# First mixer: the pool's columns of the input projection ahead of the recurrence's

## The chip, the cores and the metric

The kernel runs on one core of one Trainium2 chip. The metric is the device time of one execution in microseconds. The kernel before took 1364.03 us (median of 3 runs, 1363.72 to 1364.52).

## What is computed

Two blocks of a network work on 256 tokens of width 1024. The first block begins with a mixer of three branches, and only this mixer is touched by the change. The reference, cut to it:

```python
h = rms_norm(x, g_mix_pre[l])
(lru_x, lru_gate, pool_in, q, k, v, q_idx, k_idx, w_idx,
 gate_logits) = split_columns(h @ w_in[l], IN_SIZES)     # 512, 512, 512, 512, 64, 64, 512, 64, 8, 3072
ua = causal_depthwise_conv(lru_x, conv_w[l], conv_b[l])
ya = rg_lru(ua, ...) * jax.nn.gelu(lru_gate)             # recurrence over the tokens
yb = multiscale_pool(pool_in, w_pool[l], pool_scale[l])  # means over windows of 2, 4, 8, 16 tokens, then a 128x128 product per group
yc = dsa_attention(q, k, v, q_idx, k_idx, w_idx)         # attention over the top 64 keys
up = jnp.einsum('bsnc,ncd->bsnd', jnp.stack([ya, yb, yc], axis=2), w_branch[l])
gates = jax.nn.sigmoid(gate_logits.reshape(bsz, s, N_BRANCH, D_MODEL) + b_gate[l])
merged = jnp.sum(gates * up, axis=2)
```

Behind it come the mixer's output projection, an attention over a memory, a feed-forward part, and a second block of two layers with a token mixer and 32 experts each.

## The kernel before

The mixer is `mixer1`. The normed input stands transposed in `hT`, split into a high and a low part (`hTh`, `hTl`). Weights are loaded by SyncE's queue (SP) in tiles of 1 MB (`load_w`, L224), and each half of a tile is split into a high part by ScalarE (`whi`, L239) and a low part by VectorE (`wlo`, L241). The pool `whl` has three buffers for such a pair. `halves` hands the pairs out in the order of a list (`cols`, then `order`) and issues one split ahead. A **unit** (L287) is one product of 128 output columns: 8 × 3 matmuls of 256 tokens (L277 to L279), and a copy by ScalarE.

`main` (L532) is a generator that runs the units in order: four for the index queries `iT`, four for the queries `qT`, four for `lru_x`, four for `lru_g`, four for `poolT`, and then for each branch n in the order 1 (pool), 0 (recurrence), 2 (attention), twice: four gate units, and two products of the branch with `w_branch` (24 matmuls each, in the order of the branch's four column groups g0 to g3 or k0 to k3, for two column blocks). It yields after each.

Beside it run up to three **chains**, also generators, kept in one list: `dsa` (attention, L702), `lru` (recurrence, L827) and `pooling` (L786). After each yield of `main` the chains get one step and two steps in turn (L596); `step` (L155) always takes the chain at the head of the list and puts it at the end. `dsa` is started after the first `qT` unit, `lru` after the first `lru_g` unit, `pooling` after the last `poolT` unit. In front of the first product of a branch, `finish` (L170) steps all chains round until that branch's chain is at its end; no unit of `main` is issued in between.

One group k of `lru` is five steps: the convolution (L822, L824) and a square; the matmuls for its two gates (L856, 8 of them) and their Tanh (L860, L861); the decay (L867 to L872); a Sqrt (L875, L876); then L878, L879, the scan over the tokens (L880), L881 and the split of the result into `yh` (L882) and, at the head of the next step, `yl` (L884). The tiles `lua`, `lz`, `lr`, `li`, `la` and `lt` have one buffer each. One group g of `pooling` is g + 1 additions (L804), L811 to L813, a product (L815, two matmuls in the trace), and the split (L795, L796). `dsa` first makes scores and picks keys for both halves of the tokens, then for each half and each half of the heads: products (L759, four matmuls in the trace at a time, "quad" below), scaling (L753), a softmax (L694 to L700), transposes (L769), a product with the values (L778) and the split (L782, L784).

The framework waits and allocates by itself and orders each engine's instructions by priority in the order of the source; an instruction that isn't ready in its reckoning can be passed by later ones. The engines take their instructions in the order so made.

Of the kernel before, what the change touches and what calls it, by code (L numbers as in the profile page):

```python
# [138 lines left out]
class Net:  # L139
# [339 lines left out]
    def mixer1(self, ph):  # L479
# [5 lines left out]
        with tc.tile_pool(name="pxn", bufs=1, reuse_waits="tile") as pxn:  # L485
            xn = self.normed(pxn, "n1")
            hT = self.hpair(ph, 8)
# [5 lines left out]
        s1 = cp.enter_context(tc.tile_pool(name="ps1", bufs=1, reuse_waits="tile"))  # L493
        A4 = lambda name: s1.tile([P, 4, S], F32, name=name, tag="A4", bufs=7)
        ys = [Split(*[s1.tile([P, 4, S], F32R, name="y%s%d" % (q, n)) for q in "hl"]) for n in range(3)]
# [15 lines left out]
        for src, dst in ((kv_raw[:, :, 0:64], kT), (iw_raw[:, :, 0:64], kiT)):  # L511
            W = self.hl_tiles(KT, 128)
            for d in range(2):
# [6 lines left out]
        self.unit(W, hT, self.copy_to(vw), m=72)  # L520

        cols = ([2176 + 256 * n for n in range(2)] + [1536 + 256 * n for n in range(2)]
                + [256 * n for n in range(6)])
        order = []
        for n in (1, 0, 2):
            for half in range(2):
# [2 lines left out]
        hs = self.halves([(win[:, c:c + 256], KT, 256, "n") for c in cols] + order)  # L529
        tmp = {}  # L530

        def main():  # L532
            for j in range(4):
                self.unit(next(hs), hT, self.copy_to(iT[:, j]))
                if j == 0:
                    bk = self.bank()
                    for tt in range(2):
                        self.nc.tensor.transpose(bk[:, tt * 72:(tt + 1) * 72], vw[:, tt * P:(tt + 1) * P], self.ident[:72, :72])
                    act.activation(vtok, bk[:, :144].rearrange("p (t n) -> p t n", t=2), AF.Copy)
                yield  # L540
            for j in range(4):
                self.unit(next(hs), hT, self.copy_to(qT[:, j]))
                if j == 0:
                    tmp["dsa"] = self.start(self.dsa(s1, A4, qT, kT, iT, kiT, vtok, ys[2]))
                yield
            lru_x = s1.tile([P, 4, 3 + S], F32, name="lru_x")
            lru_g = A4("lru_g")
            poolT = s1.tile([P, 4, 16 + S], F32, name="poolT")
            v.memset(lru_x[:, :, 0:3], 0.0)
            v.memset(poolT[:, :, 0:16], 0.0)  # L550
            for j in range(4):
                self.unit(next(hs), hT, self.copy_to(lru_x[:, j, 3:]))
                yield
            for j in range(4):
                self.unit(next(hs), hT, self.copy_to(lru_g[:, j]))
                if j == 0:
                    tmp["lru"] = self.start(self.lru(s1, lru_x, lru_g, ys[0]))
                yield
            for j in range(4):
                self.unit(next(hs), hT, self.copy_to(poolT[:, j, 16:]))  # L560
                yield
            tmp["pool"] = self.start(self.pooling(s1, poolT, ys[1]))
            for n in (1, 0, 2):
                for half in range(2):
                    g = A4("gates")
                    for i in range(4):
                        j = n * 8 + half * 4 + i
                        self.unit(next(hs), hT, lambda b: act.activation(g[:, i], b, AF.Tanh, bias=bg[:, j:j + 1], scale=0.5))
                        yield
                    if half == 0:  # L570
                        self.finish(tmp[{1: "pool", 0: "lru", 2: "dsa"}[n]], fill=0)
                    for f2 in range(2):
                        W = next(hs)
                        bk = self.bank()
                        for f in range(2):
                            self.feat(bk[:, f * S:(f + 1) * S], W, f * P, P, ys[n])
                        k0 = half * 4 + f2 * 2
                        gg = g[:, f2 * 2:f2 * 2 + 2]
                        b = bk.rearrange("p (f t) -> p f t", f=2)
                        m = merged[:, k0:k0 + 2]  # L580
                        if n == 1:
                            v.scalar_tensor_tensor(m, gg, 1.0, b, op0=OP.add, op1=OP.mult)
                        else:
                            v.scalar_tensor_tensor(gg, gg, 1.0, b, op0=OP.add, op1=OP.mult)
                            v.tensor_tensor(m, m, gg, op=OP.add)
                        if n == 2:
                            if k0 == 0:
                                tmp["mT"] = self.hpair(ph, 8)
                            mT = tmp["mT"]
                            sl = slice(k0, k0 + 2)  # L590
                            act.activation(mT.hi[:, sl], m, AF.Copy, scale=0.5)
                            v.scalar_tensor_tensor(mT.lo[:, sl], m, 0.5, mT.hi[:, sl], op0=OP.mult, op1=OP.subtract)
                        yield

        for i, _ in enumerate(main()):
            self.step(1 + i % 2)  # L596
# [9 lines left out]
        with c:  # L606
            hs = self.halves(self.w_chunks(A["w_out"][0], KT))
# [1356 lines left out]
```

## Time and profile before

| | before |
|---|---|
| median of 3 runs | 1364.03 us |
| the profiled execution: its own time | 1362.82 us |
| the profiled execution: span of its instructions | 1360.9 us |
| TensorE busy (matmul) | 1246.7 us (92%) |
| VectorE busy | 702.4 us (52%) |
| ScalarE busy | 552.3 us (41%) |
| mean granted TensorE clock | 0.957 |

The span runs from the first to the last instruction. Busy time is the time in which an instruction of the engine runs; overlapping ones count once. TensorE's matmuls are pipelined, so that a busy TensorE isn't one at its peak. The mixer takes the first 220 us or so of the span, and the change touches the stretch from about 50 us on.

### The profile page before, as it was taken

How to read it: one execution, taken by the hardware profiler on the slowest of the kernel's cores; microseconds unless marked ns; L12 is line 12 of the kernel's file. 1: busy time of each engine (PE TensorE's matmuls, PEld its weight loads, DVE VectorE, ACT ScalarE, POOL GpSimd, SP SyncE). 2: the span in 40 equal slices, each digit the busy share in tenths (PEclk: the TensorE clock that was granted, in tenths of full speed). 3: DMA queues.
4: the chain of work that ended last, by engine and by line, in shares of the span. 5: the costliest groups of instructions: out<-in, count | busy, mean ns of one | idle time of the engine just before them, and what ended most of it. 6: DMA issues, size and time to landing. Idle time of an engine off the chain costs nothing. (4 is left out here: it accounts for less than half of the span.)

```text
span 1360.9 us, 26539 instructions
## 1 busy us (share of the span) xinstructions
PE 1246.7 (92%) x11058; PEld 999.5 (73%) x11058; DVE 702.4 (52%) x1414; ACT 552.3 (41%) x1022; POOL 76.8 (6%) x91
## 2 busy tenths in 40 slices
PE   6999999999999999999989977788999989978886
PEld 6988899866999995788876645465888877645553
DVE  5797756545555554686563322225685553332324
ACT  5578546544444443445532211114345532211212
POOL 2000000000000001122100000001122100000000
PEclk9998999999999998999989999888999989998988
DMA  9553448769955555864368999999563476999994
GB/s 313 166 180 96 167 159 275 303 269 379 365 201 188 186 186 180 296 228 152 142 278 364 418 418 419 418 420 336 175 229 139 171 279 281 418 418 418 418 418 181
DMA packets 131946, 375.93 MB, mean 276 GB/s; under 512 B 7056, under 2 KB 90128, under 8 KB 100848
## 3 DMA queue, kind: packets, MB, share of 16 engines
q1 hardware_dynamic: 130080, 367.84, 71.8%
q0 software_dynamic: 1312, 5.21, 1.0%
q8 instruction: 90, 1.47, 0.4%
q10 hardware_dynamic: 432, 1.14, 0.2%
q14 instruction: 32, 0.26, 0.1%
HBM read 373.12 MB, written 1.05 MB: 275 GB/s over the span
## 5 line engine op out<-in xcount | busy, mean ns | idle before, releaser
L241 DVE TENSOR_TENSOR wlo<-w,whi 128x1024 fp32r<-128x1024 f32 x214 | 263.0, 1231 | 190.0 <-ACT whi L239 189.7
L239 ACT ACTIVATE whi<-w 128x1024 fp32r<-128x1024 f32 x214 | 225.7, 1057 | 269.4 <-PE bk L278 181.2
L277 PE MATMUL bk<-hTh,whi 128*128 128x256 f32 (+1 forms) x1128 | 321.8, 287 | 2.7 <-ACT whi L239 2.5
L278 PE MATMUL bk<-hTl,whi 128*128 128x256 f32 (+1 forms) x1128 | 317.2, 282 | 0.9 <-DVE hTl L384 0.7
L279 PE MATMUL bk<-hTh,wlo 128*128 128x256 f32 (+1 forms) x1128 | 316.3, 281 | 0.3 <-DVE wlo L241 0.2
L277 PEld LDWEIGHTS bk<-hTh,whi 128*128 128x128 f32 (+1 forms) x1128 | 211.5, 188 | 21.4 <-issue 4.1
L1631 PE MATMUL bk<-w,XT 128*32 128x256 f32 (+1 forms) x2816 | 178.1, 410 | 44.9 <-DMA w<-in_w_up 41.0
L278 PEld LDWEIGHTS bk<-hTl,whi 128*128 128x128 f32 (+1 forms) x1128 | 210.9, 187 | 3.4 <-DVE hTl L384 1.2
L279 PEld LDWEIGHTS bk<-hTh,wlo 128*128 128x128 f32 (+1 forms) x1128 | 210.8, 187 | 2.0 <-DVE kk L1421 0.8
L1631 PEld LDWEIGHTS bk<-w,XT 128*32 128x32 f32 x2816 | 100.2, 118 | 121.6 <-issue 72.6
L1760 PE MATMUL bk<-Sg,xn 128*128 128x128 f32 x704 | 90.1, 285 | 4.3 <-DVE Sg L1740 4.3
L1760 PEld LDWEIGHTS bk<-Sg,xn 128*128 128x128 f32 x704 | 87.6, 201 | 6.8 <-issue 5.3
L1815 PE MATMUL bk<-w,hd 128*32 x704 | 79.8, 593 | 9.1 <-DMA w<-in_w_down 5.4
L1803 ACT ACTIVATE hd<-bk 128x256 f32<-128x256 f32 x22 | 8.4, 384 | 192.3 <-PE bk L1801 192.3
L1766 DVE TENSOR_SCALAR XT<-bk,gp,modcol 128x128 f32<-128x128 f32 x88 | 36.1, 410 | 87.3 <-PE bk L1760 79.0
L1822 ACT ACTIVATE oh<-od 128x512 fp32r<-128x512 f32 x44 | 27.7, 629 | 88.0 <-DVE od L1821 88.0
L1815 PEld LDWEIGHTS bk<-w,hd 128*32 128x32 f32 x704 | 23.4, 110 | 53.2 <-issue 49.6
L1793 DVE SCALAR_TENSOR_TENSOR mth<-mth,cslot,bk 128x256 f32<-128x256 f32 x22 | 10.6, 481 | 90.6 <-PE bk L1631 90.6
L1764 ACT ACTIVATE XT<-bk,modcol,gp 128x128 f32<-128x128 f32 x88 | 40.1, 456 | 37.0 <-DVE XT L1766 37.0
L1055 PE MATMUL ada<-w,cact 128*32 128x512 f32 x384 | 52.4, 654 | 1.0 <-DMA w<-in_w_ada 1.0
L1821 DVE TENSOR_TENSOR od<-bk,gb 128x512 f32<-128x512 f32 x44 | 30.2, 687 | 36.0 <-PE bk L1815 36.0
L1823 DVE TENSOR_TENSOR ol<-od,oh 128x512 fp32r<-128x512 f32 x44 | 30.4, 691 | 31.6 <-ACT oh L1822 31.5
(511 smaller groups left out, 1938.1 us busy)
## 6 DMA issues: line engine op xcount, KB each, us to landing
w<-in_w_gate SPq DMA_DIRECT2D x64, 1024.0 KB, 19.9
w<-in_w_up SPq DMA_DIRECT2D x64, 1024.0 KB, 19.9
w<-in_w_down SPq DMA_DIRECT2D x64, 1024.0 KB, 19.9
w<-in_w_in SPq DMA_DIRECT2D x48, 1024.0 KB, 6.6
w<-in_w_ada SPq DMA_DIRECT2D x48, 1024.0 KB, 5.0
w<-in_w_ffn_in SPq DMA_DIRECT2D x22, 1024.0 KB, 11.5
w<-in_w_out SPq DMA_DIRECT2D x12, 1024.0 KB, 5.3
w<-in_w_ffn_out SPq DMA_DIRECT2D x11, 1024.0 KB, 6.8
```

Source lines behind the costliest of these rows:

```text
L239: self.nc.scalar.activation(W.hi, v, AF.Copy)
L241: self.nc.vector.tensor_tensor(W.lo, v, W.hi, op=OP.subtract)
L277: mm(out, l.hi, r.hi, start=start, stop=False)
L278: mm(out, l.hi, r.lo, start=False, stop=False)
L279: mm(out, l.lo, r.hi, start=False, stop=stop)
L1055: te.matmul(bk[q * 32:(q + 1) * 32, :], cact[:, k:k + 1].to_broadcast([P, 32]), w[:, q * 512:(q + 1) * 512], start=k == 0, stop=k == KT - 1)
L1631: self.nc.tensor.matmul(out[ps, :S], XT[:, k, ps], w[i][:, k * S:(k + 1) * S], start=k == 0, stop=k == KT - 1)
L1760: te.matmul(o, xn[:, tt, d], Sg[:, tt], start=tt == 0, stop=tt == 1)
L1764: act.activation(XT[:, d], o, AF.Identity, scale=gp[:, d:d + 1], bias=bp[:, d:d + 1])
L1766: v.tensor_scalar(XT[:, d], o, gp[:, d:d + 1], bp[:, d:d + 1], op0=OP.mult, op1=OP.add)
L1815: te.matmul(bks[h][ps, :], hd[:, f, ps], wds[i][:, f * D + h * 512:f * D + h * 512 + 512], start=f == 0, stop=f == 1)
L1823: v.tensor_tensor(o.lo, t, o.hi, op=OP.subtract)
```

## The change

The units of the pool's columns go ahead of those of `lru_x` and `lru_g`, the columns of `w_in` are loaded in that order, and `pooling` is started between them. `lru_g` is allocated after that.

```diff
         cols = ([2176 + 256 * n for n in range(2)] + [1536 + 256 * n for n in range(2)]
-                + [256 * n for n in range(6)])
+                + [256 * n for n in (4, 5, 0, 1, 2, 3)])
...
             lru_x = s1.tile([P, 4, 3 + S], F32, name="lru_x")
-            lru_g = A4("lru_g")
             poolT = s1.tile([P, 4, 16 + S], F32, name="poolT")
             v.memset(lru_x[:, :, 0:3], 0.0)
             v.memset(poolT[:, :, 0:16], 0.0)
+            for j in range(4):
+                self.unit(next(hs), hT, self.copy_to(poolT[:, j, 16:]))
+                yield
+            tmp["pool"] = self.start(self.pooling(s1, poolT, ys[1]))
+            lru_g = A4("lru_g")
             for j in range(4):
                 self.unit(next(hs), hT, self.copy_to(lru_x[:, j, 3:]))
                 yield
...
-            for j in range(4):
-                self.unit(next(hs), hT, self.copy_to(poolT[:, j, 16:]))
-                yield
-            tmp["pool"] = self.start(self.pooling(s1, poolT, ys[1]))
             for n in (1, 0, 2):
```

## Rows read from the trace of the kernel before

**Rows 1.** Windows of 10 us: busy us of each engine, granted clock, DMA share, GB/s

```profile
core 0: us, PE busy (x) PEld busy (x) DVE busy (x) ACT busy (x) POOL busy (x), PEclk, DMA share, GB/s
90.00:100.00 10.00, 10.00 (x80) 8.99 (x80) 8.24 (x23) 6.38 (x17) 0.00 (x0) 1.00 0.47 153
100.00:110.00 10.00, 6.87 (x32) 3.52 (x31) 9.08 (x29) 6.81 (x17) 0.00 (x0) 0.64 0.26 89
```

**Rows 2.** Windows cut at the hole in TensorE's work, same columns

```profile
98.50:110.50 12.00, 8.87 (x43) 4.77 (x42) 10.13 (x34) 8.79 (x21) 0.00 (x0) 0.68 0.28 89
...
103.00:110.50 7.50, 6.70 (x28) 3.49 (x28) 6.35 (x22) 4.34 (x10) 0.00 (x0) 0.50 0.00 0
110.50:113.00 2.50, 2.50 (x13) 2.45 (x12) 1.90 (x5) 2.48 (x5) 0.00 (x0) 0.51 0.01 3
113.00:150.00 37.00, 36.93 (x308) 34.95 (x307) 28.90 (x54) 29.44 (x58) 0.56 (x1) 1.00 0.46 157
```

**Rows 3.** Timeline, TensorE around the hole: start, us, instruction, [idle before and its releaser]

```profile
95.07 0.49 PE L759 MATMUL bk<-kT,qT 64*128 64x128 f32 x4
...
98.52 0.65 PE L856 MATMUL bk<-lua,wa 64*64 64x256 f32 x4
...
99.53 0.70 PE L815 MATMUL bk<-pooled,wp 128*128 128x256 f32 x2
...
100.07 0.60 PE L769 MATMUL bk<-con,att 128*128 128x128 f32 x4
...
103.03 1.22 PE L815 MATMUL bk<-pooled,wp 128*128 128x256 f32 x2 [2.36 <-DVE pooled L813]
...
108.70 1.19 PE L815 MATMUL bk<-pooled,wp 128*128 128x256 f32 x2 [0.77 <-DVE pooled L813]
...
110.55 0.58 PE L277 MATMUL bk<-yh,whi 128*128 128x256 f32 x1
```

**Rows 4.** Timeline, VectorE: the last split of weights inside the hole

```profile
100.68 1.22 DVE L241 TENSOR_TENSOR wlo<-w,whi 128x1024 fp32r<-128x1024 f32 x1
```

**Rows 5.** Timeline, ScalarE and VectorE: the recurrence's group k1 inside the hole

```profile
99.95 0.46 ACT L860 ACTIVATE lr<-bk,hb 64x256 f32<-64x256 f32 x1
...
103.10 0.59 ACT L822 ACTIVATE lua<-lru_x,par 128x256 f32<-128x256 f32 x1
...
103.72 1.28 ACT L876 ACT_TABLE_LOAD   x1
...
105.01 0.42 ACT L876 ACTIVATE lt<-lt 128x256 f32<-128x256 f32 x1
...
107.20 0.68 DVE L880 TENSOR_TENSOR_SCAN lr<-la,lt 128x256 f32<-128x256 f32 x1
...
108.95 0.43 DVE L884 TENSOR_TENSOR yl<-lr,yh 128x256 fp32r<-128x256 f32 x1 [0.20 <-ACT yh L882]
...
111.72 0.47 ACT L860 ACTIVATE lr<-bk,hb 64x256 f32<-64x256 f32 x1
```

**Rows 6.** Timeline, ScalarE and VectorE: group k3, outside the hole, to its scan

```profile
131.67 0.46 ACT L860 ACTIVATE lr<-bk,hb 64x256 f32<-64x256 f32 x1
...
136.82 0.69 DVE L880 TENSOR_TENSOR_SCAN lr<-la,lt 128x256 f32<-128x256 f32 x1
```

**Rows 7.** Timeline, TensorE from the pool's branch to the attention's last product

```profile
120.46 0.60 PE L769 MATMUL bk<-con,att 128*128 128x128 f32 x4
...
137.88 0.70 PE L759 MATMUL bk<-kT,qT 64*128 64x256 f32 x4
...
149.94 1.03 PE L769 MATMUL bk<-con,att 128*128 128x128 f32 x8
...
152.34 0.39 PE L277 MATMUL bk<-yh,whi 128*128 128x256 f32 x1
...
167.68 1.13 PE L769 MATMUL bk<-con,att 128*128 128x128 f32 x8 [0.87 <-DVE att L700]
...
169.40 0.43 PE L778 MATMUL bk<-pT,vtok 128*64 128x128 f32 x2 [0.58 <-ACT pT L771]
170.31 1.10 PE L778 MATMUL bk<-pT,vtok 128*64 128x128 f32 x14
```

**Rows 8.** Timeline, GpSimd: issue of the pool's weights

```profile
15.17 0.75 POOL L790 DMA_DIRECT2D wp<-in_w_pool  x1 [0.97 <-DMA grow<-in_b_ada]
```

## The prediction

> **What bounds the kernel now.** I read the stage in four steps. First the windows of 10 us: up to 100 us TensorE is busy 10.00 of 10.00, and between 100 and 110 us it falls to 6.87 at a granted clock of 0.64 [rows 1]. Nothing ahead of that hole costs TensorE time, so the change can only be worth something at such holes. Second, the windows cut at the hole [rows 2]: from 98.5 to 110.5 us VectorE is busy 10.13 of 12.00 us, and TensorE's clock is at its lower level (1.2 GHz) from 103 to 113 us. Third, TensorE's order in the hole [rows 3]: the last gate unit ends at 98.52, the first matmul of the pool's branch starts at 110.55, and between them stand only small matmuls of the three chains. The longest wait, 2.36 us, is for `pooled` (L813). Fourth, the recurrence's own chain inside the hole [rows 5] and outside it [rows 6].
>
> The hole is `finish` of the pool (L571). I counted the yields: four loops of four units and the first four gate units give the chains one and two steps in turn, and pooling is started so late that 18 more steps (six of each chain) stand in TensorE's order with no gate unit between them. TensorE's order in the trace is that source order [rows 3]: recurrence group k1, pool g1, attention, pool g2 and so on. The recurrence's `finish` needs no step in the kernel before: its last group is done by then.
>
> What the hole costs: 110.55 − 98.52 = 12.0 us. The small matmuls in it need at full clock: two recurrence groups of about 1.0 (98.52 to 99.53), three pool pairs of 0.54 (99.53 to 100.07), transposes 0.60, attention products 0.6 (1.10 × 8/14 [rows 7]), two attention quads of 0.49. That is 5.8 us, so 6.2 are lost; and 110.5 to 113 us runs at half clock and gives away another 1.2 [rows 2]. **7.4 us** lie in the hole, and that is the most that the change can win there.
>
> **The change part by part.**
>
> Unit order and weights. The same twelve units run, and the six weight loads of 1 MB on SP's queue swap places among themselves. No size changes, and TensorE waits for no load here [rows 1], so I cost it at nothing; the cover is TensorE's own work, and a load that came late would cost its delay in full. The load of `wp` on POOL's queue is issued at 15.17 us [rows 8]; it may now go ahead of the loads of `wa` and `wx` on that queue, which are used some 50 us later: nothing either. `lru_g` takes a buffer of the seven of its tag later, and the number of buffers in use is the same: nothing.
>
> The pool's `finish`. Counted again with the new order, pooling has had all but one of its steps when the fourth gate unit of the pool's branch is done; `finish` needs 2 steps, not 18. TensorE stands at 98.52 plus two pool pairs that now come earlier (2 × 0.54) less one attention quad that comes later (0.49): 99.1. Then pool g3 (0.54) and the quad (0.49): 100.1. The branch's first nine matmuls need only g0 to g2, the next needs g3's `yl`. For that wait I have two ends: 0 (VectorE is ahead) and 2.36, the longest wait for `pooled` now [rows 3]. By the counted steps VectorE has about as much to do up to there as before, so I take 0.5, nearer to nothing. The branch starts, as it were, at 100.6, about 10 us earlier, and at full clock.
>
> The recurrence's `finish`. This is what is late next. The recurrence starts at the same unit of its own, but that unit now comes four units later, and nothing makes up for it: when the gate units of its branch are done, the matmuls of group k2 have only just been queued, and `finish` needs **17 steps**: nine of the recurrence (k2 from its decay to its end, and all of k3) and eight of the attention, again with no gate unit between them. The 18 steps have moved by twelve units; they have not gone.
>
> When: in the trace 110.55 to 149.94 is those twelve units and one attention round (39.4 us) [rows 3, 7]. Less 1.2 for the clock and 0.4 because the quads there are of 0.49 and not of 0.70 [rows 3, 7], 37.8. So the last gate unit ends at 100.6 + 37.8 = 138.4, and k2's first activation comes 1.4 later (98.52 to 99.95 [rows 3, 5]): 139.8.
>
> How long: the tiles `lr`, `lt` and `la` have one buffer each, so k3's first activation waits for k2's last read. A group takes from `lr` to `yl` 9.43 us in the hole (99.95 to 109.38 [rows 5]). Outside the hole the part from `lr` to the scan is 5.84 us, not 7.93 [rows 6, 5], so 7.34 is the other end. I take 8.9: VectorE loses pooling as a competitor, but the attention rows are now twice as wide. Between the groups 0 to 2.3 us: k1 ended at 109.38, and k2 began at 111.72 behind a table load. I take 1.0. So k3's `yl` comes at 139.8 + 8.9 + 1.0 + 8.9 = 158.6.
>
> On ScalarE each group changes the activation table to Sqrt and back. The row shows what that costs in line: the load follows the instruction ahead of it by 0.02 us, takes 1.28, and the Sqrt starts 0.01 later [rows 5]. This is in the 9.43.
>
> The Trainium skill (ScalarE: Activation LUTs, What ACT_TABLE_LOAD costs) gives about 1283 ns for the load, which the trace confirms, and some 1380 ns of drain on top, of which these rows show nothing. By the page an estimate for four switches would be 5.5 us more, 1373.6 instead of 1368.1.
>
> Against the trace of before: there the recurrence's branch starts at 152.34. After that point the kernel before still has to do what the new one has behind it: nine matmuls (1.1), the attention's second product (1.1 [rows 7]) and a quad (0.7), and one of two waits of TensorE (0.58 [rows 7]), while the new one runs its first 2.5 us at half clock as before (1.2). Together 2.2 in favour of the new one. Sum: 158.6 − 152.34 − 2.2 = **+4.1 us**. Later stages are shifted and not changed, so this lasts to the end.
>
> The profiled execution took 1362.82 us by its own time, with a span of 1360.9; it lies 1.2 below the median of 1364.03. Added to the median: **1368.1 us**.
>
> The ends of the unknowns: group 7.34 or 9.43, gap 0 or 2.3, wait at the pool's branch 0 or 2.36. All low is −0.6 us, all high +8.3: 1363.4 to 1372.3.
>
> **The rivals.**
>
> *The hole's matmuls are placed early* (the other side, faster). If the framework's ordering puts k2's matmuls ahead of gate units of its branch, the chain starts earlier, by 2.84 us a unit ((149.94 − 138.58) / 4 [rows 7]). It decides from 1.4 units on; 2.4 give a time 0.2% below before, three give 4.1 − 8.5 = −4.4: 1359.6. For it: one set of transposes stands a unit ahead of its place at 120.46 [rows 7]. Against it: the split of the gate unit behind the hole was done at 101.90 [rows 4], TensorE was idle to 103.03 [rows 3], and that unit was still not put into the hole. Chance 0.13.
>
> *One gate unit fills the hole, or the chain runs as fast as outside it.* A third buffer of split weights is free for one unit, worth 2.84: 1365.3. Groups at 7.34 without a gap: 1363.4 to 1364.0. Against it the same 101.90, and the 9.43 measured in a hole. Both are within 0.2%. Chance together 0.29.
>
> *The change doesn't do what it says.* VectorE, busy 10.13 of 12.00 in the hole [rows 2], doesn't finish pooling by the pool's branch, so that the first hole stays at some 6 us and the second comes on top: 1374. Against it: pooling's steps now are spread over 14 units. Chance 0.04.
>
> *Each table switch drains.* Were there 1.38 us beside each load, in rows that don't show it: 1373.6. Against it the 0.02 and 0.01 [rows 5]. Chance 0.02.
>
> *The forecast*, two groups in line in a second hole: 0.52, itself 1366.8 to 1372.3.
>
> **How the numbers follow.** A measurement of this kernel can tell about 0.2% (2.7 us) from no change. Slower: 0.52 + 0.04 + 0.02 = 0.58. Same: 0.29. Faster: 0.13. For 8 in 10 the range leaves out most of the faster rival below and the two smallest above: 1361.5 to 1372.5.
>
> **What would show it.** Right: no idle stretch of TensorE between the last gate unit of the pool's branch and that branch, at about 98 to 101 us, with the clock at 1.00; a new hole of 12 to 20 us from about 139 us, with the clock at its lower level, k2's L856 right behind the last gate unit at its head and k3's `yl` (L884) as what ends it; L860 of k3 after L884 of k2. Wrong: k2's L856 between gate units, gate units inside the second hole, a wait for `pooled` at the first, or a hole under 8 us.

## The result, and the profile after

| | before | after |
|---|---|---|
| median of 5 runs each | 1363.72 us (1362.77 to 1364.52) | 1370.97 us (1370.28 to 1371.40) |
| ratio, 95% interval | | 1.0054 (1.0043 to 1.0064) |
| the profiled execution: its own time | 1362.82 us | 1371.24 us |
| the profiled execution: span | 1360.9 us | 1369.4 us |
| mean granted TensorE clock | 0.957 | 0.951 |
| first matmul of the mixer's output projection | 216.40 us | 222.45 us |

The change is slower by 0.54%, 7.3 us of the medians; 4.1 were forecast. The last row is the first matmul behind the whole mixer. I call it the mixer's end and use it below, since it leaves out what later stages add. The row in the kernel before, then after:

```profile
216.40 0.28 PE L277 MATMUL ob<-whi,hTh 128*128 128x256 f32 x1
```

```profile
222.45 0.28 PE L277 MATMUL ob<-whi,hTh 128*128 128x256 f32 x1
```

The first hole is gone. TensorE in the kernel after, by stretches cut where its work thins out; the columns are those of [rows 1]:

```profile
core 0: us, PE busy (x) PEld busy (x) DVE busy (x) ACT busy (x) POOL busy (x), PEclk, DMA share, GB/s
98.50:110.50 12.00, 12.00 (x99) 11.39 (x98) 10.90 (x23) 9.64 (x19) 0.00 (x0) 1.00 0.37 111
...
138.60:147.70 9.10, 4.49 (x37) 2.47 (x36) 6.56 (x16) 8.03 (x14) 0.00 (x0) 1.00 0.36 116
147.70:159.70 12.00, 6.79 (x28) 4.33 (x28) 6.52 (x19) 8.43 (x22) 0.00 (x0) 0.55 0.01 1
159.70:165.50 5.80, 5.80 (x25) 4.87 (x25) 3.83 (x8) 1.72 (x3) 0.00 (x0) 0.50 0.00 0
```

The stretch of [rows 2] that was 8.87 us busy at a clock of 0.68 is now 12.00 us busy at 1.00. Instead there are 21.1 us from 138.6 to 159.7 in which TensorE works 11.3. The clock is still 1.00 in the first part, where TensorE works 4.49 of 9.10 us, and at its lower level (0.50, 1.2 GHz) for most of the second part and for 5.8 us behind it. TensorE's timeline at both places, with the idle time ahead of a row and its releaser in brackets:

```profile
99.58 0.60 PE L815 MATMUL bk<-pooled,wp 128*128 128x256 f32 x2
100.11 0.49 PE L759 MATMUL bk<-kT,qT 64*128 64x128 f32 x4
100.53 0.38 PE L277 MATMUL bk<-yh,whi 128*128 128x256 f32 x1
...
138.62 0.65 PE L856 MATMUL bk<-lua,wa 64*64 64x256 f32 x4
...
142.28 0.66 PE L778 MATMUL bk<-pT,vtok 128*64 128x128 f32 x8 [1.98 <-ACT pT L771]
...
146.59 0.65 PE L856 MATMUL bk<-lua,wa 64*64 64x256 f32 x4 [2.59 <-DVE lua L824]
...
152.38 2.02 PE L769 MATMUL bk<-con,att 128*128 128x128 f32 x8 [4.71 <-DVE att L700]
...
154.94 0.69 PE L778 MATMUL bk<-pT,vtok 128*64 128x128 f32 x2 [0.53 <-ACT pT L771]
...
159.76 0.58 PE L277 MATMUL bk<-yh,whi 128*128 128x256 f32 x1
```

The pool's branch starts at 100.53 behind the last pool product, without a wait (forecast 100.6, and 110.55 in [rows 3]). The last gate unit of the recurrence's branch ends at 138.62 (forecast 138.4). Behind it come the steps of `finish`, and the four waits, together 9.8 us, are by their releasers on both chains: on attention (L771 and L700, 7.2 us) more than on the recurrence (L824, 2.6 us).

ScalarE in the second hole, and then VectorE, both in order of time:

```profile
139.93 0.46 ACT L860 ACTIVATE lr<-bk,hb 64x256 f32<-64x256 f32 x1
...
143.75 1.28 ACT L876 ACT_TABLE_LOAD   x1
145.04 0.42 ACT L876 ACTIVATE lt<-lt 128x256 f32<-128x256 f32 x1
...
148.95 0.51 ACT L696 ACTIVATE att<-att,dsmx 128x256 f32<-128x256 f32 x1 [2.19 <-DVE dsmx L694]
...
151.05 0.49 ACT L696 ACTIVATE att<-att,dsmx 128x256 f32<-128x256 f32 x1
...
151.54 0.45 ACT L860 ACTIVATE lr<-bk,hb 64x256 f32<-64x256 f32 x1
```

```profile
147.72 1.19 DVE L694 TENSOR_REDUCE dsmx<-att 128x4 f32<-128x1024 f32 x1
...
149.89 0.43 DVE L884 TENSOR_TENSOR yl<-lr,yh 128x256 fp32r<-128x256 f32 x1 [0.64 <-ACT yh L882]
...
156.81 0.42 DVE L753 SCALAR_TENSOR_TENSOR att<-bk,bias 128x256 f32<-128x256 f32 x1 [2.50 <-PE bk L759]
...
159.13 0.42 DVE L784 TENSOR_TENSOR yl<-bk,yh 128x256 fp32r<-128x256 f32 x1 [1.56 <-ACT yh L782]
159.47 0.41 DVE L879 SCALAR_TENSOR_TENSOR lt<-li,lt 128x256 f32<-128x256 f32 x1
...
163.23 0.76 DVE L753 SCALAR_TENSOR_TENSOR att<-bk,bias 128x256 f32<-128x256 f32 x2 [1.88 <-PE bk L759]
163.90 0.42 DVE L884 TENSOR_TENSOR yl<-lr,yh 128x256 fp32r<-128x256 f32 x1
```

Group k2 runs from 139.93 to 150.31 (10.38 us), k3 from 151.54 to 164.32 (12.78 us). k3's L860 stands on ScalarE right behind the four exponentials of the attention (L696). In k3, VectorE stands idle for 2.50, 1.56 and 1.88 us ahead of attention rows (L753, L784) that wait for TensorE's products or what ScalarE makes of them, and the recurrence's L879 and L884 are queued behind these rows.

**The ledger.** Take as lost the idle stretches of TensorE over 0.4 us between 40 us and the mixer's end, and half of its busy time in the stretches at half clock. Before: 5.58 idle, and half of 6.70 + 2.50 [rows 2], 4.6: 10.2 us. After: 9.81 idle, and half of 6.79 + 5.80, 6.3: 16.1 us. The difference, 5.9, is close to the 6.05 us by which the mixer's end moved. Of the 5.58, 2.45 lie outside the first hole: three waits on the attention, 0.87 and 0.58 in [rows 7] and this one in the kernel before, none of which the kernel after has:

```profile
151.97 0.43 PE L778 MATMUL bk<-pT,vtok 128*64 128x128 f32 x2 [1.00 <-ACT pT L771]
```

So the two holes, the clock in and behind them and these three waits are all that the loss inside the mixer needs. The clock of 0.55 makes the halves slightly too large.

The other 2.4 us of the profiled pair (8.42 of own time, less 6.05) arise at two places in later stages, which the change doesn't touch. The first is this one, with the next row of ScalarE that waits for TensorE there; before, then after, same columns:

```profile
320.00:330.00 10.00, 8.51 (x80) 3.82 (x76) 7.72 (x13) 6.20 (x12) 0.71 (x1) 0.83 1.09 358
...
331.53 1.35 ACT L383 ACTIVATE hTh<-bk,par 128x256 fp32r<-128x256 f32 x3 [3.05 <-PE bk L378]
```

```profile
326.00:336.00 10.00, 8.51 (x69) 3.61 (x64) 7.79 (x13) 6.20 (x12) 0.71 (x1) 0.69 1.08 358
...
338.88 1.35 ACT L383 ACTIVATE hTh<-bk,par 128x256 fp32r<-128x256 f32 x3 [4.34 <-PE bk L378]
```

TensorE is busy for the same time, with fewer matmul records (69 for 80) and the clock at 0.69 instead of 0.83. Counted from the mixer's end, ScalarE's row comes at 115.13 us before and at 116.43 after, 1.3 later. In the kernel with two buffers below, the clock at this place is 1.00 and the row comes at 113.59, behind a wait of 1.54:

```profile
324.70:334.70 10.00, 8.51 (x90) 4.28 (x83) 7.74 (x13) 6.20 (x12) 0.71 (x1) 1.00 1.09 358
...
334.73 1.35 ACT L383 ACTIVATE hTh<-bk,par 128x256 fp32r<-128x256 f32 x3 [1.54 <-PE bk L378]
```

So the wait grows as the clock falls. The second place adds about as much: from 550 to 560 us the clock was 1.00, and from 556 to 566 us in the kernel after it is 0.83.

### The profile page after: what moved, and what is told of

Its sections match the earlier page's. It is cut to its first block, busy times and chain, and to the rows that moved or that the text cites. A ratio compares the mean times of both kernels' runs of the same rounds, so it can differ in the third digit from the quotient of the medians.

```text
span 1369.4 us, 26542 instructions
## 1 busy us (share of the span) xinstructions
PE 1253.0 (91%) x11058; PEld 1004.6 (73%) x11058; DVE 702.5 (51%) x1414; ACT 552.9 (40%) x1022; POOL 76.3 (6%) x91
## 3 DMA queue, kind: packets, MB, share of 16 engines
q8 instruction: 90, 1.47, 0.4%
## 5 line engine op out<-in xcount | busy, mean ns | idle before, releaser
L1631 PE MATMUL bk<-w,XT 128*32 128x256 f32 (+1 forms) x2816 | 181.1, 415 | 43.5 <-DMA w<-in_w_up 39.6
```

The source lines that it names most:

```text
L1631: self.nc.tensor.matmul(out[ps, :S], XT[:, k, ps], w[i][:, k * S:(k + 1) * S], start=k == 0, stop=k == KT - 1)
```

## The experiments

Theory: the steps that the unit order doesn't cover come back at the next `finish`, where two dependent chains take turns in line and TensorE idles and loses its clock. Rivals: the recurrence's own length sets the hole (one buffer a tile, table loads); the half clock sets it; the new order of the units is itself worse. "Mixer's end" is as above; before 216.40, after 222.45. It is read from each kernel's one profile, while the time is the median of its runs. The runs of one kernel lie up to 9 us apart (two buffers: 1362.41 to 1371.25), and the two profiles of the kernel after have the mixer's end at 222.45 and 221.66, so differences of the mixer's end below about 1 us aren't read. Kernels with added lines have their line numbers moved by two to seven.

| kernel | time, us | ratio to before (95%) | mixer's end, us |
|---|---|---|---|
| after, again | 1370.96 | 1.0063 (1.0044 to 1.0082) | 221.66 |
| new order, finish steps its own chain | 1363.84 | 1.0001 (0.9988 to 1.0014) | 219.57 |
| old order, finish steps its own chain | 1362.73 | 1.0003 (0.9992 to 1.0015) | 216.54 |
| new order, pooling started late | 1366.44 | 1.0023 (1.0007 to 1.0038) | 219.38 |
| two buffers for a group's tiles | 1365.59 | 1.0035 (1.0016 to 1.0053) | 221.14 |
| no table switch | 1370.28 | 1.0062 (1.0036 to 1.0089) | 222.32 |
| own chain and no table switch | 1362.70 | 0.9998 (0.9987 to 1.0009) | 216.53 |
| useless matmuls in the hole | 1368.78 | 1.0049 (1.0030 to 1.0067) | 220.37 |
| due chain first | 1373.84 | 1.0076 (1.0050 to 1.0101) | 226.86 |
| **new order, each chain once per unit** | **1353.54** | 0.9933 (0.9911 to 0.9955) | 206.80 |
| old order, each chain once per unit | 1360.92 | 0.9984 (0.9974 to 0.9994) | 215.96 |

### The order alone

```diff
-            tmp["pool"] = self.start(self.pooling(s1, poolT, ys[1]))
             lru_g = A4("lru_g")
...
+            tmp["pool"] = self.start(self.pooling(s1, poolT, ys[1]))
             for n in (1, 0, 2):
```

> The new order of units and columns alone; pooling is started behind the last lru_g unit, as late as in the kernel before. Counted steps of finish: 18 for the pool, 4 for the recurrence. Theory A (the time follows the steps that stand in finish): the first hole is that of the kernel before, about 12 us from 98.5, and a short one of about 5 us stands before the recurrence's branch: 1366 to 1368. Theory C (the order of columns and weights is what costs): as the changed kernel, 1370 to 1372, with waits for weights. If neither, as before: 1363.7.

The first hole is back where it was, with the waits on pooling's VectorE steps:

```profile
104.86 1.19 PE L815 MATMUL bk<-pooled,wp 128*128 128x256 f32 x2 [1.72 <-DVE pooled L813]
109.62 1.22 PE L815 MATMUL bk<-pooled,wp 128*128 128x256 f32 x2 [3.57 <-DVE pooled L813]
```

The mixer's end comes 3.0 us later than in the kernel before, and 3.1 us earlier than with pooling queued early. The time, 1366.44, is what theory A expected, and theory C's 1370 to 1372 didn't come. So the early start does remove the first hole, and within this way of stepping it costs more than it wins: the steps that pooling takes early are taken from the recurrence. (Counted steps in the two `finish`: 18 and 4 here, 2 and 17 in the kernel after.)

### Finish steps only its own chain, in both orders

```diff
         while any(g in self.chains for g in gens):
+            if not fill:
+                self.chains.sort(key=lambda c: c not in gens)
             self.step(1)
```

> The changed kernel, but finish steps only the chain that it waits for: the recurrence's nine steps stand in the second hole, and the attention's eight come later, between units. Theory A (the hole is two groups of the recurrence in line): the hole still opens behind the last gate unit at about 138.6 us; without the attention's instructions a group takes 7.3 us as outside a hole, plus a table load of 1.3 between them, so k3's yl comes at about 156 instead of 164.3 and the branch's first matmul at about 148 to 156. Some 5 us of TensorE work leaves the hole and is paid later, so the time falls by about 3 us: 1367 to 1369. Theory B (the attention's instructions in VectorE's order make the hole long, the recurrence alone is short): a hole under 10 us and 1364 or less.

> The old order of the units; a finish now steps only its own chain. Counted: 6 steps of pooling alone at the pool's branch, 5 of the recurrence at its own, where there were 18 of three chains and none. Theory (steps put off come back at the next finish): the first hole shrinks from 12.0 us to 5 to 8, a second of some 5 us opens at the recurrence's branch, and the first w_out matmul stays within 2 us of the kernel before (216.4 us): 1361 to 1365 us. Rival: the steps of other chains in the first finish were pure loss, and none come back: first w_out matmul at 209 to 212 us, time 1355 to 1358 us.

In the new order the attention leaves the hole, and the groups take 7.68 and 8.30 us, inside the two ends of the forecast (7.34 and 9.43). TensorE still waits twice behind the last gate unit, and a gate unit of the next branch now stands there too:

```profile
144.06 1.12 PE L858 MATMUL bk<-lua,wa 64*64 64x256 f32 x4 [4.83 <-DVE lua L826]
...
151.96 1.12 PE L780 MATMUL bk<-pT,vtok 128*64 128x128 f32 x8 [1.99 <-ACT pT L773]
...
154.17 0.58 PE L279 MATMUL bk<-hTh,whi 128*128 128x256 f32 x1
```

The first wait is for the recurrence, the second for the attention's `pT`, whose row on ScalarE (L773) stands behind k3's activations. Both marks of theory B came, a hole under 10 us (the branch starts 7.8 us behind k2's first matmul) and a time of 1364 or less; theory A's 1367 to 1369 didn't. But not all of that is the mixer's: its end is 2.9 us earlier than after, and by the time of runs it is 7.1 us; from the mixer's end to the end of the span the profile has 1143.0 us, against 1147.0 in the kernel after.

In the old order the pool's branch starts 4.0 us earlier than before (106.57 instead of 110.55), and the mixer's end doesn't move (216.54): the steps left out of the first `finish` come back as waits at the recurrence's branch (1.47 us from 155.24, less than the 5 us expected) and in the attention (1.86 us from 178.52). The theory's expectation of the mixer's end and the time held, and the rival that the other chains' steps are pure loss fell.

### What ends the second hole: buffers and table loads

Two buffers for the tiles that keep k3 waiting, and one fewer of the tag `A4` to make room; and, in another kernel, a Tanh in the place of the Sqrt, which needs no other table and changes the recurrence's values:

```diff
-        A4 = lambda name: s1.tile([P, 4, S], F32, name=name, tag="A4", bufs=7)
+        A4 = lambda name: s1.tile([P, 4, S], F32, name=name, tag="A4", bufs=6)
...
-        T = lambda n: pool.tile([P, S], F32, name="l" + n)
+        T = lambda n: pool.tile([P, S], F32, name="l" + n, bufs=2 if n in ("r", "i", "a", "t") else 1)
```

> The changed kernel with two buffers for lr, li, la and lt, paid for by six buffers instead of seven of the tag A4. Theory A (the hole is as long as two groups in line): k3's first activation no longer waits for k2's yl; it may start behind k3's own matmuls at 148 instead of 151.5, so the branch starts about 3 us earlier, 1367 to 1369. Rival (the order on VectorE and TensorE's slow attention products set the end): 1370 to 1372.

```diff
-            act.activation(t, t, AF.Sqrt)
+            act.activation(t, t, AF.Tanh)
```

> The changed kernel with Tanh in place of the recurrence's Sqrt, which stands in another activation table; this changes the recurrence's values, and its time shows what the table loads cost in the second hole. By the row (1.28 us a load, nothing beside it) the load ahead of each Sqrt leaves the line of each group: 2 x 1.28, so output projection about 2.6 us earlier than 222.4, 1368 to 1369. Were there a drain of 1.38 us beside each load, 5 us or more: 1366 or less. If the loads are hidden, 1371.

Seen from the first matmul of group k2 (138.62 in the kernel after), in us:

| kernel | k3's L860 | attention's transposes, L769 | branch starts | k3's `yl` done | mixer's end |
|---|---|---|---|---|---|
| after | 12.9 | 13.8 | 21.1 | 25.7 | 83.8 |
| two buffers | 9.1 | 14.1 | 21.2 | 25.8 | 83.4 |
| no table switch | 10.4 | 15.0 | 21.7 | 20.1 | 84.6 |
| useless matmuls | 13.3 | 14.1 | 21.1 | 22.8 | 81.6 |
| own chain | 10.4 | outside | 7.8 | 18.7 | 81.4 |
| own chain, no table switch | 9.4 | outside | 8.2 | 16.4 | 79.1 |

With two buffers k3 starts 3.8 us earlier, and nothing behind it moves. That is no shorter recurrence: only the first of k3's four activations (L860, L861) went ahead of the attention's exponentials, and its `yl` comes at 25.8 as before. TensorE's longest wait is again for the attention:

```profile
151.78 0.45 PE L769 MATMUL bk<-con,att 128*128 128x128 f32 x1 [5.04 <-DVE att L700]
```

Without the table switch the recurrence is done 5.6 us earlier, and the branch starts 0.6 us later, since k3's L860 and L861 now go ahead of the attention's exponentials on ScalarE. TensorE and VectorE in that kernel:

```profile
152.71 2.02 PE L769 MATMUL bk<-con,att 128*128 128x128 f32 x8 [4.55 <-DVE att L700]
```

```profile
157.40 0.43 DVE L884 TENSOR_TENSOR yl<-lr,yh 128x256 fp32r<-128x256 f32 x1
```

k3's `yl` is there at 157.83, and the branch starts at 159.48 all the same: ahead of it in TensorE's order stand the attention's transposes, products and quads, all behind a softmax that is late. So the attention ends the hole here, not the recurrence. The time without the switch, 1370.28, is near the 1371 expected if the loads are hidden. That two buffers brought the time to 1365.59, which neither theory nor rival expected, isn't explained by the mixer, where it won 0.4 us behind k2's first matmul. The profiled run, 1362.68 us and one of the fastest of eight, has the rest in later stages (from the mixer's end to the end of the span 1139.6 us, against 1147.0 in the kernel after).

If so, the table loads must count once the attention is out:

> New order; a finish now steps only its own chain, and the recurrence's Sqrt is a Tanh, so that its activation table is not switched (the recurrence's values change by this). Theory: with the attention's eight steps out of the hole the recurrence's two groups end it, so what a group saves counts in full. A group took 7.68 and 8.30 us in e1_after_own and holds one table load of 1.28 us ahead of its Sqrt; without it k3's yl comes about 2.5 us earlier (154.3 us instead of 156.85), the first w_out matmul at about 217 us instead of 219.57, time some 1361 us. Rival: something else than the recurrence ends the hole (the gate unit that stands in it, the attention's steps behind it): yl earlier, first w_out matmul still at 219 to 220 us, time 1363 to 1365 us.

They do: k3's `yl` comes 2.3 us earlier, TensorE no longer waits for `pT`, and from k2's first matmul to the mixer's end it is 79.1 us instead of 81.4, 2.3 less, where the theory said about 2.5 and its rival none. By the time of runs it is 1.1 (1362.70; the theory said some 1361, the rival 1363 to 1365), which doesn't decide. So without the attention's steps the recurrence's length counts, by the mixer's end of one profile each.

### The clock

Four useless products behind every step of `finish`:

```diff
             self.fill(fill)
+            if not fill:
+                bk = self.bank()
+                for k in range(4):
+                    self.nc.tensor.matmul(bk[:, :S], self.warm.hi[:, k, :P], self.warm.hi[:, k], start=k == 0, stop=k == 3)
...
+        self.warm = hT
```

> The changed kernel with four extra matmuls of 256 tokens, whose result nobody reads, after each step of finish (about 0.47 us of TensorE a step at full clock, 8 us in the second hole). What it prices is the clock. Theory: the granted clock stays nearer to 1.00 in the hole and behind it; the 6 us at half clock behind the hole cost 3 us and the slowed attention products in it another 1 to 2, so 1366 to 1368. If the clock is of no account, or falls all the same, 1371 or a little more.

The two stretches that ran at 0.55 and 0.50, and k3's last row:

```profile
147.70:159.70 12.00, 9.47 (x76) 7.43 (x75) 7.58 (x21) 8.33 (x22) 0.00 (x0) 1.00 0.01 1
159.70:165.50 5.80, 5.80 (x42) 4.88 (x41) 4.30 (x9) 1.46 (x2) 0.00 (x0) 1.00 0.00 0
```

```profile
161.10 0.42 DVE L889 TENSOR_TENSOR yl<-lr,yh 128x256 fp32r<-128x256 f32 x1 [0.48 <-ACT yh L887]
```

With the clock at 1.00 throughout, k3 takes 9.43 us instead of 12.78, and the mixer's end comes 2.1 us earlier. Median 2.2 us below after, 1368.78, just above the 1366 to 1368 expected. The branch starts no earlier (21.1 in the table), but this doesn't clear the clock of the hole's length: between the attention's transposes (152.84) and the branch (159.90) stand 24 of the useless matmuls, some 3.7 of 7.1 us by their starts, where the kernel after takes 7.4 us at half clock (152.38 to 159.76) without them. What the clock gave back there, the useless matmuls took. What the run shows is the tail behind the hole.

### The steps spread differently

First the chain that is due next gets three of four steps:

```diff
-            self.step(1 + i % 2)
+            for half in range(2):
+                due = [tmp[c] for c in ("pool", "lru", "dsa") if tmp.get(c) in self.chains]
+                if due and i % 2 and half:
+                    due.reverse()
+                self.chains.sort(key=lambda c: c not in due[:1])
+                self.step(1)
```

> The changed kernel with other steps between units: two after every unit; three of four go to the chain whose branch comes first (pool, then recurrence, then attention), each fourth to the attention first. Counted steps of finish: none for all three branches. Theory A: neither hole is there; of the kernel before's 7.4 us in the first hole all is won and the changed kernel's second hole is gone: about 1356 (1354 to 1358). Rival: the chains' instructions are late on VectorE, which is busy 8 to 9.5 of 10 us there, whatever the order of steps, so that TensorE waits in smaller pieces: 1360 to 1364.

Both expectations were missed, and in the other direction. The time, 1373.84, is above the kernel after. TensorE now idles in ten places, 13.66 us in all. Two of them:

```profile
125.29 0.65 PE L861 MATMUL bk<-lua,wa 64*64 64x256 f32 x4 [2.18 <-DVE lua L829]
```

```profile
144.09 1.06 PE L774 MATMUL bk<-con,att 128*128 128x128 f32 x4 [2.12 <-DVE att L705]
```

With the steps of one chain one right behind the other, a unit of 2.84 us [rows 7] is not long enough for what VectorE and ScalarE have to do between two of its matmuls. By the count no step was left for a `finish`; they were too close together. The next kernel tests this reading.

Then each chain one step after each unit, the recurrence one more after every fourth, and `finish` with its own chain alone:

```diff
+            if not fill:
+                self.chains.sort(key=lambda c: c not in gens)
             self.step(1)
...
-            self.step(1 + i % 2)
+            mine = [tmp[c] for c in ("lru", "pool", "dsa") if tmp.get(c) in self.chains]
+            if i % 4 == 3 and tmp.get("lru") in self.chains:
+                mine.append(tmp["lru"])
+            for c in mine:
+                self.chains.sort(key=lambda g: g is not c)
+                self.step(1)
```

> The changed kernel, with every chain stepped once after each unit, the recurrence once more after each fourth, and finish stepping its own chain alone. Counted steps of finish: none for all three. Theory A with what the run with two steps a unit taught (dependent steps of one chain must not stand in one unit, or TensorE waits in small pieces): no hole, and no wait over 1 us but for the attention's: TensorE comes to the output projection some 7 us earlier than in the kernel before (216.4), at 208 to 211, and the time is 1355 to 1359. Rival (VectorE's load keeps TensorE waiting whatever the steps): idle pieces of over 8 us in all, 1362 or more.

```profile
90.00:100.00 10.00, 10.00 (x85) 9.21 (x85) 10.00 (x27) 8.94 (x16) 0.00 (x0) 1.00 0.45 157
100.00:110.00 10.00, 10.00 (x86) 9.74 (x85) 9.13 (x21) 9.39 (x22) 0.00 (x0) 1.00 0.36 117
...
140.00:150.00 10.00, 10.00 (x82) 9.20 (x81) 7.47 (x11) 5.57 (x13) 0.00 (x0) 1.00 0.62 206
150.00:160.00 10.00, 10.00 (x93) 9.69 (x92) 6.39 (x11) 5.17 (x10) 0.00 (x0) 1.00 0.61 210
```

Counted, no `finish` has a step left. From 40 us to the mixer's end TensorE has no idle stretch over 0.4 us, and the clock is at 1.00 in all these rows. Median 1353.54 us (1352.69 to 1354.07): faster than both kernels, by 0.67% than before, and better than theory A expected (1355 to 1359, mixer's end 208 to 211). It also checks the ledger: 216.40 less the 10.2 lost before would be 206.2, and 222.45 less 16.1 would be 206.4; measured 206.80. VectorE is busy 8.1 to 10.0 of 10 us from 80 to 140.

The same stepping in the old order:

> The same stepping in the kernel before, its order of units kept. Counted steps of finish: 4 for the pool (its own), none for the others. Theory A: a hole of four pool steps in line, some 5 us instead of 12, at 98 us, and none later: output projection at 211 to 214, 1358 to 1361. It tells whether the changed order of units is worth anything once the steps are spread: by theory A 2 to 3 us beside the run with the changed order.

```profile
106.47 0.67 PE L822 MATMUL bk<-pooled,wp 128*128 128x256 f32 x2 [1.82 <-DVE win L813]
110.73 1.19 PE L822 MATMUL bk<-pooled,wp 128*128 128x256 f32 x2 [3.59 <-DVE pooled L820]
```

The hole at the pool's branch stays (6.9 us of waits on pooling from 98.6 on), and the mixer ends at 215.96, not at 211 to 214 as expected. That pooling's input comes too late for any stepping is argued; VectorE's load, 13.48 of 14.00 us from 98 to 112, isn't separated from it. So the order of the change is worth 9.2 us there (215.96 to 206.80), 7.4 by the medians, once the steps are spread so that the second hole doesn't open, where 2 to 3 were expected; with the stepping as it was, the same order costs 6.05.

### The kernel after, again

> The changed kernel as it is, beside the two above. 1369.5 to 1372 us, first w_out matmul at 222.3 to 222.6 us; from there to the end of the span 1143 to 1148 us, if that part varies from run to run by itself; 1146 to 1148 us, if the change makes it longer.

The distances in the second hole agree with the first profile to 0.01 us, the mixer's end comes 83.63 instead of 83.83 us behind k2's first matmul, and the clock in the later stretch is low again. The row of that stretch:

```profile
326.00:336.00 10.00, 8.51 (x72) 3.89 (x72) 7.05 (x12) 5.93 (x12) 0.71 (x1) 0.66 1.08 361
```

The mixer's end itself, 221.66, is 0.6 us earlier than expected, since k2's first matmul already comes 0.6 us earlier than in the first profile (138.03). From the mixer's end to the end of the span it is 1147.1 us (1147.0 in the first profile, 1144.5 in the one of before). So the longer later part came twice with this kernel. The two expectations overlap there (1143 to 1148, 1146 to 1148), so this doesn't show that the change makes it longer: the new order with late pooling, too, has 1146.9.

## Why the prediction was right or wrong

**Right: where the hole goes.** The direction, the disappearance of the first hole, the start of the pool's branch (100.53 for 100.6), the head of the new hole (138.62 for 138.4) and k2's L860 (139.93 for 139.8) came as forecast, and with them the count of 2 and 17 steps. The wait for the pool's g3, taken as 0.5 between 0 and 2.36, was 0 for the matmuls.

**The sum by its terms.** Forecast: 158.6 − 152.34 − 2.2 = +4.1. Measured in the profiled pair: the branch starts at 159.76, 7.42 behind the 152.34 of [rows 7]; from there to the mixer's end it takes 62.69 us against 64.06, 1.37 less; together 6.05. So the first part was 1.2 too low and the second 0.8 too favourable, and the later stages, forecast at nothing, added 2.4. That the sum came this near is in part luck, as the next paragraph shows.

**Wrong: what ends the hole.** The step "k3's `yl` comes at 158.6" named the recurrence as the end. `yl` came at 164.32, 5.7 us later, and the branch started at 159.76 without waiting for it: two errors that nearly cancelled. The hole was 21.1 us long, beyond the 12 to 20 forecast. The groups were mis-sized: 10.38 and 12.78 us, not 8.9 and 8.9, above the upper end of 9.43, which came from a hole where the attention's rows were half as wide (at a clock of 1.00, in the kernel with useless matmuls, k3 took 9.43). And `yl` of k3 is not what the branch's first nine matmuls wait for; they need k0 to k2, as I had said of the pool's branch and not carried over to this one. What held them was the attention, eight of the 17 steps, which I had counted and given no duration: its softmax is late by VectorE's and ScalarE's order, and TensorE takes its transposes and products in line. The kernel without the table switch shows it, since it shortens the recurrence by 5.6 us and not the hole; so does the one whose `finish` leaves the attention out, where the branch starts 13 us sooner behind k2's first matmul. How much of the hole's end is the attention's rows at half clock is open: by the ledger half of 6.79, 3.4 us. With the attention out, the effect of the table loads shows that the recurrence's length then counts. The gap was 1.23 for 1.0.

**Mis-sized: the clock.** I gave the stretch behind the hole 2.5 us at half clock, worth 1.2, as before. It was 5.8 us long, worth 2.9. The useless matmuls won 2.1 us at the mixer's end with the clock at 1.00.

**Not foreseen: the later stages.** "Shifted and not changed, so this lasts to the end" held for the work and not for its time: 2.4 us in the profiled pair. It lies in lower granted clock at two places. In the eleven profiles of the experiments that part takes 1139.6 to 1149.4 us without any change to it, so by an estimate from these a forecast from the mixer alone is good to some 3 to 5 us. What makes the clock fall for longer in one profile than in another stays open. One kernel's runs spread as widely (before, 20 runs of one set: 1358.20 to 1364.67), and only the kernel after was profiled twice.

**The rivals.** No matmul of k2 was placed early: its L856 stands right behind the last gate unit. No gate unit entered the hole in the kernel after, but one did as soon as the attention had left it. No drain is seen at the table switch: the Sqrt starts 0.01 us behind its load (143.75 + 1.28, 145.04), and without the attention the two groups save 2.3 us, less than two loads. So what the Trainium skill states of a drain of some 1380 ns beside the load (ScalarE: Activation LUTs, What ACT_TABLE_LOAD costs) isn't seen in this kernel.

## What to carry to other kernels

When helper chains are interleaved with a long stream of matmuls, count the steps that are left at every point where a chain must be complete, not only at the one that is being mended: steps given to one chain are taken from another, and they return at the next such point. In this kernel it paid to spread the steps, one step of each chain behind each long unit (the recurrence had a second behind every fourth), and not to favour the chain that is due; the same reordering cost 7 us with the stepping as it was and, beside the old order under the same spread stepping, won 7. For the length of such a hole, price every chain in it, and look at which of them TensorE waits for last.

## What the runs showed of the hardware that wasn't expected

Half clock on TensorE lengthens chains whose own work is on VectorE: k3 took 12.78 us at a granted clock of 0.55 and 0.50, and 9.43 at 1.00, and the rows show the recurrence's steps on VectorE behind rows that wait for slow matmuls. With some useless matmuls in the idle time the clock stayed up (1.00 for 0.55), and the kernel's median was 2.2 us lower with more work in it. And stretches at half clock in stages that an edit doesn't touch became longer (0.83 to 0.69 in 10 us): the whole later part took 2.4 us more, of 8.42 between the profiled executions.
